# The end of a mixture-of-experts kernel: row blocks of the last weights, and one 1/rms chain for both token blocks

## The chip, the cores and the metric

One core of a Trainium2 chip runs the whole program. The metric is device time in microseconds, as the median of several runs. The profile is of one execution; its times count from the start of its span.

## The reference, cut to what matters

A layer of a language model on 256 tokens of 1024 features, all in float32: a mixer (mLSTM and differential attention), then a mixture of 32 experts, then a final RMS norm. The change touches only the end:

```python
for e in range(N_EXPERTS):                       # 32 experts, 512 hidden features each
    hid = jax.nn.silu(t @ w_eg[e]) * (t @ w_eu[e])
    out = out + gates[:, e:e + 1] * (hid @ w_ed[e])
x = x + out
return rmsnorm(x, normf_g)                       # x * rsqrt(mean(x*x) + eps) * g
```

## The kernel before, in words

All expert weights (32 times 6 MB) stream through SBUF slots of 1 MB. An expert sees only the tokens routed to it: their columns are gathered, multiplied, and the result is added back by a "scatter" matmul with a 0/1 matrix `S_l` into four PSUM banks `acc[j][t]` (j: the half of the 1024 features, t: the block of 128 tokens). These banks hold the sum over all experts and the residual.

Experts are worked on in groups of two or four. A group of four shares the 128 output partitions, 32 slots for each expert. The last group has four, and its down weights `w_ed` are the last thing loaded: 8 MB. Each expert's down weights lie in two slots, `hf` 0 and 1; a slot holds two weight rows k for each partition (k = 2 hf and 2 hf + 1), each of 1024 columns. `load_by_columns` (L776) loads them in pieces: for hf 0 and then hf 1 the first 512 columns of both rows (512 KB for each expert), then for hf 0 the other 512 columns of both rows, then for hf 1 the other 512 columns of row 2 and at last of row 3 (256 KB for each expert and row). All loads are issued on SP's queue (L784), in that order.

On TensorE `down` (L914) multiplies, for the rows `ks` and the halves `js` that it is given, row by row and in a row expert by expert. `keep_warm` (L189) issues matmuls whose result nobody reads. `last_down` (L1132) does for one half j: the rows in pieces with such matmuls between them, then the copy `oH` of the result on ScalarE (L1140), the difference `oL` on VectorE (L1141) and the scatter of both into `acc[j][0]` and `acc[j][1]` (L1144).

Then comes the norm. `square` (L1110, ScalarE) sums the squares of a bank into `ss`; `gain` (L1114, VectorE) writes the bank times the norm's vector `nfb` into `zt`; `rms` (L1117) adds the two halves of a token block and calls `rstd_of` (L161 to L167), a chain of seven small steps between VectorE and ScalarE that gives 1/rms; `scale` (L1123 to L1128) multiplies a quarter of the result with it and issues its write. In the kernel before there is a chain for each token block. The quarter (1, 1) is worked out straight from PSUM in one instruction (L1125). The order of instructions on each engine is set when the kernel is built, by a planner that goes by its own estimate of when an instruction is ready and passes one that isn't; `issue_after` puts an instruction behind a given one of the same engine.

Of the kernel before, what the change touches and what calls it, by code (L numbers as in the profile page):

```python
# [16 lines left out]
OP = mybir.AluOpType  # L17
# [4 lines left out]
NT = 2  # L22
# [15 lines left out]
NWA, NWB, NWZ = 6, 11, 6  # L38
NPJ = 4
NST = 4  # L40
NWARM, NW1, NW2, NW3, NW5 = 9, 2, 10, 4, (8, 4, 4, 3)
NL = 3


# [60 lines left out]
def kernel(ctx: ExitStack, tc: tile.TileContext,  # L105
# [51 lines left out]
    def rstd_of(ss, n, scale, eps, tag="rs"):  # L157

        v, r, y = (cp.tile([P, n], F32, name=tag + c, tag=tag + c, bufs=2 if tag == "rs" else 1) for c in "vry")
        o = cp.tile([P, n], F32, name=tag + "o", tag=tag + "o", bufs=6 if tag == "rs" else 1)  # L160
        behind[1] = V.tensor_scalar(v, ss, scale, eps, op0=OP.mult, op1=OP.add)  # L161
        A.activation(r, v, AF.Ln)  # L162
        behind[0] = A.activation(r, r, AF.Exp, scale=-0.5)  # L163
        V.scalar_tensor_tensor(y, r, -1.0, r, op0=OP.mult, op1=OP.mult)  # L164
        V.tensor_scalar(r, r, 0.5, None, op0=OP.mult)  # L165
        V.tensor_tensor(y, y, v, op=OP.mult)  # L166
        V.scalar_tensor_tensor(o, y, 3.0, r, op0=OP.add, op1=OP.mult)  # L167
        return o
# [12 lines left out]
    def keep_warm(n, pw, after=None):  # L181

        wide = warm[:, None, :].to_broadcast([P, 4, P])
        for _ in range(n):
            if after is None:
                T.matmul(pw, warm, wide, start=True, stop=True)
            else:
                with tc.issue_after(after.ins):
                    after = T.matmul(pw, warm, wide, start=True, stop=True)  # L189
# [586 lines left out]
    def load_by_columns(src, rows):  # L776

        w = [[slot() for _ in rows] for _ in range(2)]
        for hf, k0, k1, j in ((0, 0, 2, 0), (1, 0, 2, 0), (0, 0, 2, 1), (1, 0, 1, 1), (1, 1, 2, 1)):
            for v, e in zip(w[hf], rows):  # L780
                at = [a.rearrange("p (k c) -> p k c", k=2)[:, k0:k1, j * 512:(j + 1) * 512]
                      for a in (v, of_expert(src, e)[:, hf * 2048:(hf + 1) * 2048])]
                with tc.issue_after(loaded[0].ins):
                    loaded[0] = SY.dma_start(*at)  # L784
        return w
# [121 lines left out]
    def down(ws, hT, ojs, ks=range(4), js=range(2)):  # L907
        n = len(ws) // 6
        cap = P // n
        for k in ks:  # L910
            for j in js:
                for i in range(n):
                    c0 = (k % 2) * D + j * 512
                    down_end[0] = T.matmul(ojs[j][i * cap:(i + 1) * cap], hT[:, k, i * cap:(i + 1) * cap],  # L914
                             ws["d", i, k // 2][:, c0:c0 + 512], start=(k == 0), stop=(k == 3))
        return ojs
# [191 lines left out]
    def square(j, t):  # L1108
        sq = mp.tile([P, KD, P], F32, name="xg", tag="xg", bufs=1).rearrange("p k s -> p (k s)")[:, :FF]
        A.activation(sq, acc[j][t], AF.Square, accum_out=ss[:, t, j:j + 1])  # L1110
# [2 lines left out]
        js = slice(j * 512, (j + 1) * 512)  # L1113
        V.tensor_tensor(zt[t][:, js], acc[j][t], nfb[:, js], op=OP.mult)  # L1114

    def rms(t):
        V.tensor_tensor(ss[:, t, 0:1], ss[:, t, 0:1], ss[:, t, 1:2], op=OP.add)  # L1117
        return rstd_of(ss[:, t, 0:1], 1, 1.0 / D, EPS)

    def scale(t, i, E, rf):  # L1120
        z = zt[t][:, i * 512:(i + 1) * 512]
        if E is A:
            A.activation(z, z, AF.Copy, scale=rf)  # L1123
        elif i and t:
            V.scalar_tensor_tensor(z, acc[i][t], rf, nfb[:, i * 512:(i + 1) * 512], op0=OP.mult, op1=OP.mult)  # L1125
        else:
            V.tensor_scalar(z, z, rf, None, op0=OP.mult)  # L1127
        (A if E is A else SY).dma_start(dap(out, t * P * D + i * 512, [[D, P], [1, 512]]), z)  # L1128

    last_end = [up_end[0]]  # L1130

    def last_down(j, pieces):  # L1132
        end = None
        for ks, n in pieces:
            with tc.issue_after((end or last_end[0]).ins):
                down(ws, hT_l, oj, ks, (j,))
                end = down_end[0]
            if n:
                keep_warm(n, warm_to, end)
        A.copy(oH[j], oj[j])  # L1140
        V.tensor_tensor(oL[j], oj[j], oH[j].bitcast(F32), op=OP.subtract)  # L1141
        for o_ in (oH, oL):
            for t in range(NT):
                last_end[0] = T.matmul(acc[j][t], S_l[:, t * P:(t + 1) * P], o_[j], start=False, stop=(o_ is oL),  # L1144
                                       skip_group_check=True)

    last_down(0, (((0, 1), NW5[0]), ((2, 3), 0)))
    for t in range(NT):
        square(0, t)
        gain(0, t)  # L1150
    keep_warm(NW5[1], warm_to, last_end[0])
    last_down(1, (((0, 1), NW5[2]), ((2,), NW5[3]), ((3,), 0)))
    square(1, 0)
    rf = rms(0)
    with tc.issue_after(behind[1].ins):
        gain(1, 0)
    square(1, 1)
    scale(0, 0, V, rf)
    scale(0, 1, V, rf)
    rf = rms(1)  # L1160
    scale(1, 0, A, rf)
    scale(1, 1, V, rf)


# [26 lines left out]
```

## Time and profile before

| | us |
|---|---|
| median of 3 runs | 597.77 (597.15 to 598.19) |
| profiled execution | 597.43 |
| its span | 595.6 |
| last piece of down weights there | 584.17 |
| last output product ends | 591.82 |
| mean granted clock of TensorE | 0.971 |

The span goes from the first to the last record; the time of the execution is 1.8 us longer. The stretch that matters here is the last 30 us: the last loads, the last two down products, the norm and the four writes of 256 KB.

### The profile page before, as it was taken

To read this page: it belongs to the slowest core of one execution; us is meant where nothing else is said; L and a number is where in the kernel's file an instruction comes from. 1 tells how busy PE (TensorE), PEld (TensorE's weight loads), DVE (VectorE), ACT (ScalarE), POOL (GpSimd) and SP (SyncE) were. 2 spreads that over 40 slices of the span, in tenths; PEclk is the share of its full clock that TensorE was granted. 3 is DMA by queue.
4 is the path that set the end of the run, shared out by engine and by line. 5 is a ranking of instruction groups with operands and counts; after the bars stand their busy time and mean duration, and the time that the engine had idled before them with its cause. 6 is when DMAs were issued, how large, how long until landed. Compare 5 with 4: busy or idle time off the path is not lost. (4 is left out here: it accounts for less than half of the span.)

```text
span 595.6 us, 8111 instructions
## 1 busy us (share of the span) xinstructions
PE 529.3 (89%) x3054; PEld 268.4 (45%) x3054; DVE 163.2 (27%) x472; ACT 124.7 (21%) x291; POOL 9.7 (2%) x19
## 2 busy tenths in 40 slices
PE   8999999998999999999889798579798879897683
PEld 6898779795453424343323434123432322431131
DVE  4774788845130202020200200100200010110022
ACT  6675476662100000101001000001000000010032
POOL 0000004001000000000000000000000000000000
PEclk9999999999999999999989989999987889989997
DMA  8955799969899999999999999999999999999992
GB/s 303 389 169 131 239 408 385 388 268 352 300 372 419 390 401 419 419 417 420 419 421 419 420 418 419 423 418 419 419 421 420 419 419 421 419 419 419 406 376 106
DMA packets 42876, 223.77 MB, mean 376 GB/s; under 512 B 3796, under 2 KB 6228, under 8 KB 19156
## 3 DMA queue, kind: packets, MB, share of 16 engines
q1 hardware_dynamic: 42548, 222.89, 93.6%
q8 instruction: 25, 0.41, 0.3%
q10 hardware_dynamic: 288, 0.35, 0.2%
q14 instruction: 15, 0.12, 0.1%
HBM read 221.39 MB, written 1.84 MB: 375 GB/s over the span
## 5 line engine op out<-in xcount | busy, mean ns | idle before, releaser
L897 PE MATMUL pmm<-w,xg 128*32 128x512 f32 (+1 forms) x1024 | 198.8, 615 | 21.8 <-DMA w<-in_w_eu_dram 15.7
L897 PEld LDWEIGHTS pmm<-w,xg 128*32 128x32 f32 (+1 forms) x1024 | 50.9, 122 | 139.6 <-issue 95.1
L914 PE MATMUL pmm<-w,oL 128*32 128x512 f32 (+1 forms) x448 | 97.0, 644 | 11.5 <-ACT oL L836 6.1
L914 PEld LDWEIGHTS pmm<-w,oL 128*32 128x32 f32 (+1 forms) x448 | 29.4, 130 | 71.7 <-issue 47.4
L233 DVE TENSOR_TENSOR wl<-w,wh 128x512 fp32r<-128x512 f32 (+1 forms) x72 | 44.4, 628 | 26.4 <-ACT wh L232 24.0
L843 DVE TENSOR_TENSOR oL<-pmm,oH 128x512 fp32r<-128x512 f32 x20 | 13.8, 692 | 134.2 <-PE pmm L914 104.9
L232 ACT ACTIVATE wh<-w 128x512 fp32r<-128x512 f32 (+1 forms) x72 | 40.8, 580 | 30.2 <-PE pj L263 13.1
L816 PEld LDWEIGHTS pmm<-Gm,x1c 128*128 128x128 f32 x352 | 40.6, 192 | 14.4 <-PE pmm L897 7.7
L816 PE MATMUL pmm<-Gm,x1c 128*128 128x128 f32 x352 | 43.8, 280 | 0.5 <-DVE ctr L989 0.5
L842 ACT CAST oH<-pmm 128x512 fp32r<-128x512 f32 x20 | 11.7, 585 | 120.9 <-PE pmm L914 95.7
L263 PE MATMUL pj<-hL,wh 128*128 128x256 f32 x128 | 36.0, 286 | 0.3 <-DVE hL L245 0.3
L264 PE MATMUL pj<-hH,wl 128*128 128x256 f32 x128 | 35.3, 287 | 0.0
L261 PE MATMUL pj<-hH,wh 128*128 128x256 f32 x128 | 35.3, 286 | 0.0
L817 DVE TENSOR_TENSOR xg<-pmm,cb 128x512 f32<-128x512 f32 (+1 forms) x24 | 15.0, 645 | 72.5 <-PE pmm L897 60.7
L836 ACT COPY oL<-pmm 128x512 f32<-128x512 f32 x10 | 5.8, 585 | 134.7 <-PE pmm L833 134.7
L904 ACT ACTIVATE oL<-pmm,rg 128x512 f32<-128x512 f32 x10 | 6.9, 687 | 91.5 <-PE pmm L897 67.1
L263 PEld LDWEIGHTS pj<-hL,wh 128*128 128x128 f32 x128 | 24.1, 188 | 0.6 <-DVE hL L245 0.5
L264 PEld LDWEIGHTS pj<-hH,wl 128*128 128x128 f32 x128 | 23.6, 188 | 1.4 <-issue 1.2
L261 PEld LDWEIGHTS pj<-hH,wh 128*128 128x128 f32 x128 | 23.8, 189 | 0.2
L833 PE MATMUL pmm<-ca,oH 128*128 128x128 f32 x44 | 7.2, 289 | 16.2 <-DVE oH L829 16.2
L829 DVE SCALAR_TENSOR_TENSOR oH<-oL,rg,pmm 128x512 f32<-128x512 f32 x10 | 11.2, 1119 | 25.8 <-PE pmm L897 22.7
L833 PEld LDWEIGHTS pmm<-ca,oH 128*128 128x128 f32 x44 | 5.0, 150 | 22.3 <-issue 20.1
(344 smaller groups left out, 486.3 us busy)
## 6 DMA issues: line engine op xcount, KB each, us to landing
w<-in_w_eg_dram SPq DMA_DIRECT2D x64, 1024.0 KB, 19.8
w<-in_w_eu_dram SPq DMA_DIRECT2D x64, 1024.0 KB, 19.8
w<-in_w_ed_dram SPq DMA_DIRECT2D x56, 1024.0 KB, 19.8
w<-in_w_in_dram SPq DMA_DIRECT2D x10, 1024.0 KB, 14.9
w<-in_w_ed_dram SPq DMA_DIRECT2D x12, 512.0 KB, 13.0
w<-in_w_out_dram SPq DMA_DIRECT2D x4, 1024.0 KB, 12.8
w<-in_w_ed_dram SPq DMA_DIRECT2D x8, 256.0 KB, 7.3
w<-in_w_in_dram SPq DMA_DIRECT2D x3, 512.0 KB, 7.8
```

The lines of the kernel that those rows point to most:

```text
L232: A.activation(wh, raw, AF.Copy)
L233: V.tensor_tensor(wl, raw, wh.bitcast(F32), op=OP.subtract)
L261: T.matmul(om, wh[:, cs], hH[:, k], start=(k == 0 and m % 2 == 0), stop=False, skip_group_check=True)
L263: T.matmul(om, wh[:, cs], hL[:, k], start=False, stop=False, skip_group_check=True)
L264: T.matmul(om, wl[:, cs], hH[:, k], start=False, stop=(k == KD - 1), skip_group_check=True)
L816: T.matmul(px_[:, i * P:i * P + n], x1c[:, t, k0 + i], G_[:, t], start=(t == 0), stop=(t == NT - 1))
L817: V.tensor_tensor(xg[:, k0:k0 + per, :n], px_.rearrange("p (k s) -> p k s", k=4)[:, :per, :n], cb[:, B_N2 + k0:B_N2 + k0 + per, None].to_b ...
L833: T.transpose(pt[:, k * P:k * P + n], hid[:n, k], ident[:n, :n])
L842: A.copy(oH[:n], oj[:n])
L843: V.tensor_tensor(oL[:n], oj[:n], oH[:n].bitcast(F32), op=OP.subtract)
L897: up_end[0] = T.matmul(p_[i * cap:(i + 1) * cap], xg[:, k, i * cap:(i + 1) * cap], ws[n_, i, k // 4][:, k4 * FF:(k4 + 1) * FF], start=(k = ...
L914: down_end[0] = T.matmul(ojs[j][i * cap:(i + 1) * cap], hT[:, k, i * cap:(i + 1) * cap], ws["d", i, k // 2][:, c0:c0 + 512], start=(k == 0 ...
```

## The change

The last down weights come in another order: rows 0 and 1 (hf 0) whole, 1 MB for each expert; then for hf 1 the first 512 columns of both rows (512 KB each), the other 512 columns of row 2 and those of row 3 (256 KB each). That is 16 issues in place of 20.

On TensorE the order becomes: rows 0 and 1 of half 0, 8 warming matmuls, rows 0 and 1 of half 1, 8 warming matmuls, rows 2 and 3 of half 0, row 2 of half 1, the scatter of half 0, row 3 of half 1, the scatter of half 1. The kernel before did all of half 0 with its scatter and then half 1, with 8, 4, 4 and 3 warming matmuls.

In the norm, `gain` is written ahead of `square` for each bank, the sums of both token blocks are added in one instruction, and one chain of two columns gives both 1/rms. All four quarters are scaled from `zt`: three on VectorE, one on ScalarE. `rms` and the product straight from PSUM go.

```diff
-NWARM, NW1, NW2, NW3, NW5 = 9, 2, 10, 4, (8, 4, 4, 3)
+NWARM, NW1, NW2, NW3, NW5 = 9, 2, 10, 4, (8, 8)
...
-        for hf, k0, k1, j in ((0, 0, 2, 0), (1, 0, 2, 0), (0, 0, 2, 1), (1, 0, 1, 1), (1, 1, 2, 1)):
+        for hf, k0, k1, c0, c1 in ((0, 0, 2, 0, D), (1, 0, 2, 0, 512), (1, 0, 1, 512, D), (1, 1, 2, 512, D)):
             for v, e in zip(w[hf], rows):
-                at = [a.rearrange("p (k c) -> p k c", k=2)[:, k0:k1, j * 512:(j + 1) * 512]
+                at = [a.rearrange("p (k c) -> p k c", k=2)[:, k0:k1, c0:c1]
...
-    def rms(t):
-        V.tensor_tensor(ss[:, t, 0:1], ss[:, t, 0:1], ss[:, t, 1:2], op=OP.add)
-        return rstd_of(ss[:, t, 0:1], 1, 1.0 / D, EPS)
...
-        elif i and t:
-            V.scalar_tensor_tensor(z, acc[i][t], rf, nfb[:, i * 512:(i + 1) * 512], op0=OP.mult, op1=OP.mult)
...
+    def last_down(ks, js, after, n=0):
+        with tc.issue_after(after.ins):
+            down(ws, hT_l, oj, ks, js)
+        if n:
+            keep_warm(n, warm_to, down_end[0])
+        return down_end[0]
+
+    def last_parts(j):
         A.copy(oH[j], oj[j])
         V.tensor_tensor(oL[j], oj[j], oH[j].bitcast(F32), op=OP.subtract)
...
+    def last_scatter(j, after):
+        with tc.issue_after(after.ins):
+            for o_ in (oH, oL):
+                for t in range(NT):
+                    e = T.matmul(acc[j][t], S_l[:, t * P:(t + 1) * P], o_[j], start=False, stop=(o_ is oL),
+                                 skip_group_check=True)
+        return e
+
+    e = last_down((0, 1), (0,), up_end[0], NW5[0])
+    e = last_down((0, 1), (1,), e, NW5[1])
+    e = last_down((2, 3), (0,), e)
+    last_parts(0)
+    e = last_down((2,), (1,), e)
+    e = last_scatter(0, e)
+    e = last_down((3,), (1,), e)
+    last_parts(1)
     for t in range(NT):
+        gain(0, t)
         square(0, t)
-        gain(0, t)
...
+    last_scatter(1, e)
+    for t in range(NT):
+        gain(1, t)
+        square(1, t)
+    V.tensor_tensor(ss[:, :, 0], ss[:, :, 0], ss[:, :, 1], op=OP.add)
+    rf = rstd_of(ss[:, :, 0], NT, 1.0 / D, EPS)
+    for t, i, E in ((0, 0, V), (1, 0, A), (0, 1, V), (1, 1, V)):
+        scale(t, i, E, rf[:, t:t + 1])
```

## Rows read from the trace of the kernel before

**Rows 1.** The page's second part: load rate in 40 equal slices of the span.
```profile
GB/s 303 389 169 131 239 408 385 388 268 352 300 372 419 390 401 419 419 417 420 419 421 419 420 418 419 423 418 419 419 421 420 419 419 421 419 419 419 406 376 106
```

**Rows 2.** Windows; after each engine's busy time: PE clock, DMA share, GB/s.
```profile
554.00:556.00 2.00, 2.00 (x20) 0.56 (x12) 0.00 (x0) 0.00 (x0) 0.00 (x0) 1.00 1.02 422
...
574.00:576.00 2.00, 2.00 (x17) 0.42 (x16) 0.00 (x0) 0.00 (x0) 0.00 (x0) 1.00 1.05 388
```

**Rows 3.** SP's queue by time: start, us of issuing, load issued.
```profile
562.75 0.55 SPq L784 DMA_DIRECT2D w<-in_w_ed_dram  x1
...
573.45 0.33 SPq L784 DMA_DIRECT2D w<-in_w_ed_dram  x1
...
578.85 0.33 SPq L784 DMA_DIRECT2D w<-in_w_ed_dram  x1
```

**Rows 4.** TensorE by time, gate and up products; in brackets the wait before.
```profile
452.91 6.51 PE L897 MATMUL pmm<-w,xg 128*32 128x512 f32 x28 [1.45 <-DMA w<-in_w_eg_dram]
...
552.66 3.63 PE L897 MATMUL pmm<-w,xg 128*32 128x512 f32 x28 [1.46 <-DMA w<-in_w_eu_dram]
...
562.68 3.62 PE L897 MATMUL pmm<-w,xg 128*32 128x512 f32 x26 [1.48 <-DMA w<-in_w_eu_dram]
```

**Rows 5.** The chain that ended last, by time: start, us, what.
```profile
570.41 1.92 PE pmm L914 x16
572.33 1.83 PE pmm L189 x8
...
581.89 1.00 PE pmm L914 x8
```

**Rows 6.** TensorE by time: the scatters, and the wait for the last load.
```profile
576.73 1.46 PE L1144 MATMUL acc<-w,S__3781 128*128 128x512 f32 x4 [0.70 <-ACT w L1140]
577.45 0.30 PEld L1144 LDWEIGHTS acc<-w,S__3781 128*128 128x128 f32 x2 [0.43 <-DVE w L1141]
...
584.17 0.14 PEld L914 LDWEIGHTS pmm<-w 128*32 128x32 f32 x2 [0.46 <-DMA w<-in_w_ed_dram]
...
585.90 1.46 PE L1144 MATMUL acc<-w,S__3781 128*128 128x512 f32 x4 [0.67 <-ACT w L1140]
```

**Rows 7.** ScalarE and VectorE by time: copy, squares, gains, the power chains, scales.
```profile
577.99 0.60 ACT L1110 ACTIVATE xg<-acc 128x512 f32<-128x512 f32 x1 [1.32 <-PE acc L1144]
...
578.71 1.41 DVE L1114 TENSOR_TENSOR w<-acc,w 128x512 f32<-128x512 f32 x2 [1.31 <-ACT xg L1110]
...
585.26 0.58 ACT L1140 CAST w<-pmm 128x512 fp32r<-128x512 f32 x1 [5.86 <-PE pmm L914]
...
587.22 0.60 ACT L1110 ACTIVATE xg<-acc 128x512 f32<-128x512 f32 x1 [1.38 <-PE acc L1144]
587.72 0.19 ACT L1110 ACTIVATION_READ_ACCUMULATOR xg<-acc 128x1 f32 x1
...
588.14 0.15 DVE L161 TENSOR_SCALAR rsv<-ss 128x1 f32<-128x1 f32 x1
...
589.07 0.15 DVE L161 TENSOR_SCALAR rsv<-ss 128x1 f32<-128x1 f32 x1
...
589.25 0.20 ACT L162 ACTIVATE rsr<-rsv 128x1 f32<-128x1 f32 x1 [0.29 <-DVE rsv L161]
...
589.63 0.88 DVE L1127 TENSOR_SCALAR w<-w,rso 128x512 f32<-128x512 f32 x2
...
591.07 0.72 ACT L1123 ACTIVATE w<-w,rso 128x512 f32<-128x512 f32 x1 [1.38 <-DVE rso L167]
```

**Rows 8.** The output: issues on SP's queue, and two windows as in rows 2.
```profile
590.15 0.82 SPq L1128 DMA_DIRECT2D out_dram<-w  x2
...
591.85 0.33 SPq L1128 DMA_DIRECT2D out_dram<-w  x1
```
```profile
591.00:591.50 0.50, 0.00 (x0) 0.00 (x0) 0.46 (x2) 0.43 (x1) 0.00 (x0) 0.50 0.98 360
...
593.50:594.00 0.50, 0.00 (x0) 0.00 (x0) 0.00 (x0) 0.00 (x0) 0.00 (x0) 0.50 1.05 389
```

More of the change, by code (lines that the diff above doesn't have):

```diff
@@ L1128, in scale @@
         (A if E is A else SY).dma_start(dap(out, t * P * D + i * 512, [[D, P], [1, 512]]), z)
[L1130 to L1139, printed above, removed]
+    def last_down(ks, js, after, n=0):
[4 more added lines that the diff above has]
+        return down_end[0]
@@ L1140, in last_down @@
+    def last_parts(j):
         A.copy(oH[j], oj[j])
         V.tensor_tensor(oL[j], oj[j], oH[j].bitcast(F32), op=OP.subtract)
[L1142 to L1147, printed above, removed]
+    def last_scatter(j, after):
[5 more added lines that the diff above has]
+        return e
@@ L1148 @@
+    e = last_down((0, 1), (0,), up_end[0], NW5[0])
[6 more added lines that the diff above has]
+    last_parts(1)
     for t in range(NT):
+        gain(0, t)
         square(0, t)
-        gain(0, t)
[L1151 to L1162, printed above, removed]
+    last_scatter(1, e)
[6 more added lines that the diff above has]
+        scale(t, i, E, rf[:, t:t + 1])
 _BIG = ["x", "w_in", "w_out", "w_eg", "w_eu", "w_ed"]
```

## The prediction, made before the result

> **What bounds the kernel now.** I read the page's load rate first, then the issues on SP's queue with the transfer rate beside them, then TensorE by time, then the chain that ended last, and at the end ScalarE, VectorE and the output. The load rate stays near 419 GB/s for most of the span and sags only in the last slices [rows 1]: the kernel is a stream of weights, and only what follows the stream can be shortened by work on the engines.
>
> SP issues a load when the load eight places earlier has landed, so its issue times are landing times. The last 1 MB piece of the up weights landed at 562.75; the eighth 512 KB piece of the last down weights at 573.45 and the twelfth at 578.85 [rows 3]. That is 10.70/8 = 1.34 us a piece, then 5.40/4 = 1.35: about 388 GB/s, as the window at 574 shows, against 422 for the 1 MB pieces at 554 [rows 2]. The 1 MB pieces have 8 KB in one run for each partition, the column pieces 2 KB. The last piece landed at 584.17, where TensorE's weight load waited for it [rows 6]; the last matmul of the down product ended 1.07 us later, just ahead of the copy at 585.26 [rows 7].
>
> From the copy on, the time is a chain of single steps: copy, difference and scatter (first square at 587.22, 1.96 behind the copy), square, variance (588.14), power, scales (589.63), then the output [rows 7]. The four 256 KB writes move at about 380 GB/s [rows 8]: data from 591.0, 0.85 behind the first issue, and, with the same 0.85 behind the last issue at 591.85 and 512 KB at that rate, to about 594.1.
>
> **The loads.** Rows 0 and 1 of each of the four experts now come as 1 MB, 8 KB for each partition. At the rate of the up weights, 422 GB/s [rows 2], 1.049 MB takes 2.48 us; from 562.75 on the four land at 565.2, 567.7, 570.2 and 572.7. Half columns of rows 2 and 3 follow at 1.35: 578.1. The rest is unchanged in size, 584.17 - 578.85 = 5.32 for 2 MB [rows 3, 6], so row 2 lands at about 580.8 and the last piece at 583.4. Gain: 573.45 - 572.66 = 0.79 us at the end of the loads. Bounds: 0 if long runs bring nothing here, 0.8 if they move as the up weights do; I take 0.79, since size and run are those of the rows that show it. The Trainium skill's page "DMA: Bandwidth & Descriptors" (Specifications) says that from 512 B on a transfer runs at line rate; by that the gain would be 0. The trace differs: 388 against 422 GB/s.
>
> **TensorE.** The first pass needs row 0 of all four experts before row 1, so what it needs first was complete at 562.75 + 4 x 1.34 = 568.1 before and is now at 572.66, and TensorE, which starts at 570.41 [rows 5], waits for it. In the up product, once the last expert's piece was there at 562.68, its four weight rows took 3.62 us [rows 4], so two take 1.81: 574.47. Then, each from the chain [rows 5]: 8 warming matmuls 1.83 (576.30), the pass over the other half 1.92 (578.22), 8 warming 1.83 (580.05), rows 2 and 3 of the first half 1.92 (581.97, weights there since 578.1), row 2 of the second half 1.00 (582.97, weights 580.8). The copy and the difference of the first half lie under that pass. The scatter took 1.46 with 0.43 of waiting for the difference [rows 6]; without the wait 1.03: 584.00. Row 3 takes 1.00: 585.00. By the loads alone it could end at 583.40 + 1.07 = 584.47, so now TensorE decides, and of the 0.79 only 0.24 is left beside the 585.24 of before. The copy could start at 585.02.
>
> **What gets in the way of the copy.** Scatter of the first half ahead of row 3 means that gain and square of the first half fall just where the copy is due. The first gain can start 0.89 behind the scatter's start (1.32 from the scatter's 585.90 to the square at 587.22, less 0.43 [rows 6, 7]): 583.86. A gain and a square of the same block do not run together: the first gain at 578.71 waited for the square, started at 577.99, to end, and two gains took 1.41 [rows 7]. With gain first: gain 583.86 to 584.55, square 584.58 to 585.27. ScalarE's next is either the copy or the second square. The order that is built isn't the written one: the second block's variance step ran at 589.07, ahead of the first block's scales at 589.63, which are written first [rows 7]; so an instruction that is ready passes one that isn't. Taken at the times just worked out, the first square is ready (584.58) before the copy (585.02), and at 585.27 both copy and second square are, of which the copy is written first. I take that middle order: copy at 585.29, as before (585.26). Bounds: 585.02 with the copy first, 586.01 with both squares first.
>
> **The tail, counted from the copy.** The scatter is unchanged: block 0 ready at 1.96. Gain 1.98 to 2.67 (0.69 each), second gain to 3.37, second square 3.40 to 4.09: the gain's 0.70 now lies ahead of each square, where a square came first before. Variance at 4.32 (0.23 behind the square's end, as 588.14 behind 587.91 [rows 7]). From variance to scales the first block took 1.49 (588.14 to 589.63), but its logarithm was late: a free ScalarE takes it up 0.18 behind the variance (589.07 to 589.25), that is at 588.32, and here the other square's 0.60, begun at about 587.93, held it to 588.53. Without these 0.2 it is 1.30 [rows 7]: scales at 5.62. Before, they began at 4.37. Two columns in place of one cost nothing: these steps are 0.15 to 0.2 us whatever they hold. The longer chain is covered by nothing.
>
> What is given back: no second chain, and the three products on VectorE are 0.44 each (0.88 for two), the last ending at 6.94 beside 6.56 before; ScalarE's 0.72 is off the path. The writes: the first was issued 0.52 behind the scales' start, and data flowed 0.85 later [rows 7, 8]. Before, two writes went out while the second chain ran and two after it. Now all four follow one another within 0.9 us, so the rate decides: 5.62 + 0.52 + 0.85 + 2.77 (1 MB at 380 GB/s) = 9.76, against 594.1 - 585.26 = 8.84. Tail: +0.92. If the writes overlapped fully, the bound is the last issue at about 7.0 and its 2.25 to the end of data: 9.25, +0.4.
>
> **Sum**, against the profiled execution (span 595.6, time 597.43): copy +0.03, tail +0.92, so +0.95 to 598.4. That execution lies 0.34 below the median of the three runs (597.77), so about 598.7 as a median. A difference under 0.2% (1.2 us) can't be told from none, so this counts as no change.
>
> **Rivals.**
> *The copy first* (15%): the copy at 585.02, +0.7, 598.5. For it: it is the earlier one in the text. Against it: it must be ready within 0.7 us of the first gain.
> *Both squares first* (22%), the one on the other side: the copy at 586.01, 0.75 later than before, +1.7, 599.4. It decides from a copy later than about 585.55. For it: if the order is built with TensorE's row 3 a little later than I have it, by a load or by the matmuls, the second square is ready first. Against it: at the times of this trace the copy is ready 0.25 us before the second square.
> *The long runs bring nothing* (10%): all from the first pass on is 0.79 later, since TensorE's chain hangs on the fourth expert: +1.7, 599.5. The page's rule above would give this. Against it: rows 2.
> *TensorE's clock falls while it waits for the fourth expert* (5%): one idle stretch of about 1.3 us. Once, behind a wait of 1.45, the same 28 matmul records took 6.51 in place of 3.63 [rows 4], 2.9 more; +3.8, 601.6. Against it: behind waits as long at 552.66 and 562.68 they ran at full speed [rows 4].
> *Gain and square run together* (5%): the tail loses 0.72, +0.2, 598.0. Against it: rows 7. The page "PSUM — Partial Sum Buffer" (Terms) of the Trainium skill says that two engines on one bank at once is an error, reads included; the wait at 578.71 agrees.
> *Something of the stream that I don't see gets shorter* (3%): faster by more than 1.2 us would need the loads to end 2 us earlier and TensorE to follow; nothing in the rows offers that.
>
> **Numbers.** The forecast has 40%. Its own range, 598.2 to 599.2, comes from 0.3 us on each of the scatter, the scales' start and the writes. Slower by over 0.2% are most of the both-squares case, the long-runs case, the clock's, and a fifth of the forecast's: 0.40. Faster 0.04, the same 0.56. For 8 in 10, the range goes from below the lower cases (597.6) to above both squares and the long runs (599.9), and leaves out the clock.
>
> **What would show it.** On SP's queue: four issues of 1 MB, and the last landing near 583.4. On TensorE: a wait of about 1.3 us for the fourth expert's rows and none for a load after it, last down product ending near 585.0. On ScalarE: square, copy, square. A scale start 5.6 behind the copy; four writes without a gap. The prediction is wrong if TensorE still waits for the last load, if the first pass doesn't wait, or if the writes hide behind the chain.

## The result, and the profile after

| | before | after |
|---|---|---|
| median, us | 597.77 (597.15 to 598.27, 7 runs) | 601.0 (599.17 to 602.96, 7 runs) |
| profiled execution, us | 597.43 | 599.17 |

The ratio is 1.0051 (95%: 1.003 to 1.0073): slower, and above the range that was given. The profiled execution is the shortest of its seven. By itself it is 1.74 us longer than the one before, 0.29%. So there are two differences to explain: 1.74 us between two profiles, and the 1.83 us by which the median lies above its own profile.

The page of after, the load rate in 40 slices, which answers [rows 1]:

```profile
GB/s 297 389 178 134 220 409 387 391 270 345 307 376 417 386 424 419 416 419 420 419 419 421 421 419 419 421 420 420 417 421 419 421 417 421 419 421 419 421 333 71
```

The slice of 406 before is now at 421, and the last two are lower (333 for 376, 71 for 106): the stream keeps its rate longer and is over sooner. SP's queue by time (start, us of issuing, load) and two windows of after, for [rows 2, 3]:

```profile
572.60 0.33 SPq L784 DMA_DIRECT2D w<-in_w_ed_dram  x1
...
577.95 0.33 SPq L784 DMA_DIRECT2D w<-in_w_ed_dram  x1
```

```profile
572.00:574.00 2.00, 1.38 (x10) 0.38 (x10) 0.00 (x0) 0.00 (x0) 0.00 (x0) 1.00 1.04 374
574.00:576.00 2.00, 2.00 (x10) 0.70 (x8) 0.00 (x0) 0.00 (x0) 0.00 (x0) 1.00 1.06 391
```

The fourth expert's rows landed at 572.60, and at 577.95 the 6 MB were there that had been there at 578.85 [rows 3]. In the first window TensorE is busy 1.38 of 2 us, the wait for the fourth expert; its clock stays at 1.00, the level of 2.4 GHz.

TensorE by time, after. In brackets the wait and its releaser:

```profile
562.62 3.62 PE L897 MATMUL pmm<-w,xg 128*32 128x512 f32 x26 [1.44 <-DMA w<-in_w_eu_dram]
...
572.62 1.90 PE L914 MATMUL pmm<-w 128*32 128x512 f32 x10 [1.21 <-DMA w<-in_w_ed_dram]
...
582.69 1.37 PE L1139 MATMUL acc<-w,S__3781 128*128 128x512 f32 x4
583.99 1.06 PE L914 MATMUL pmm<-w 128*32 128x512 f32 x8
586.52 1.46 PE L1139 MATMUL acc<-w,S__3781 128*128 128x512 f32 x4 [1.47 <-ACT w L1132]
```

Row 3 of the second half ran 583.99 to 585.05 without a wait: TensorE, not the loads, sets the end of the down product. Then the scatter waits 1.47 us for the copy on ScalarE, where it waited 0.67 before [rows 6]. ScalarE and VectorE by time, after (for [rows 7]):

```profile
584.59 0.60 ACT L1110 ACTIVATE xg<-acc 128x512 f32<-128x512 f32 x1 [2.04 <-DVE w L1114]
...
585.31 0.60 ACT L1110 ACTIVATE xg<-acc 128x512 f32<-128x512 f32 x1
...
585.89 0.58 ACT L1132 CAST w<-pmm 128x512 fp32r<-128x512 f32 x1
588.57 0.60 ACT L1110 ACTIVATE xg<-acc 128x512 f32<-128x512 f32 x1 [2.09 <-DVE w L1114]
...
589.28 0.60 ACT L1110 ACTIVATE xg<-acc 128x512 f32<-128x512 f32 x1
```

```profile
583.87 1.29 DVE L1114 TENSOR_TENSOR w<-acc,w 128x512 f32<-128x512 f32 x2 [0.59 <-PE acc L1139]
...
587.78 1.29 DVE L1114 TENSOR_TENSOR w<-acc,w 128x512 f32<-128x512 f32 x2 [0.59 <-PE acc L1139]
...
590.20 0.17 DVE L161 TENSOR_SCALAR rsv<-ss 128x2 f32<-128x2 f32 x1
...
591.53 1.28 DVE L1121 TENSOR_SCALAR w<-w,rso 128x512 f32<-128x512 f32 x3
```

Both squares of the first half stand ahead of the copy, which could have started at about 585.07 and starts at 585.89. The writes, after (for [rows 8]):

```profile
592.04 1.37 SPq L1122 DMA_DIRECT2D out_dram<-w  x3
...
592.28 0.36 ACTq L1122 DMA_DIRECT2D out_dram<-w  x1
```

To compare executions, I count from one event that the change doesn't touch, called the anchor: the last up weights are there and the last 26 matmuls of the up product start, at 562.68 before [rows 4] and 562.62 after. From there:

| us behind the step ahead | before | after |
|---|---|---|
| anchor to copy of the second half | 22.58 | 23.27 |
| copy to first scales | 4.37 | 5.64 |
| first scales to the execution's time | 7.80 | 7.64 |
| anchor to the execution's time | 34.75 | 36.55 |

So +0.69, +1.27, -0.16: 1.80 in all, less 0.06 for the anchor itself. A difference of 0.3 us between two profiles can also come from loads that land later: the kernel before with a steady up product (below) does the same work behind the anchor and takes 35.06.

### The profile page after: what moved, and what is told of

Same layout as the page of the kernel before. It is cut to its first block, busy times and chain, and to the rows that moved or that the text cites. A ratio compares the mean times of both kernels' runs of the same rounds, so it can differ in the third digit from the quotient of the medians.

```text
span 597.4 us, 8086 instructions
## 1 busy us (share of the span) xinstructions
PE 531.8 (89%) x3051; PEld 269.6 (45%) x3051; DVE 162.9 (27%) x467; ACT 124.3 (21%) x289; POOL 9.2 (2%) x19
## 4 chain that ended last, share of the span: by engine, by line
DMA 58%; PE 37%; DVE 2%; ACT 1%; issue 1%; SPq 0%; DVEq 0%; ACTq 0%
DMA w<-in_w_eu_dram 20%; DMA w<-in_w_ed_dram 20%; DMA w<-in_w_eg_dram 17%; PE pmm L897 8%; PE pmm L914 4%; PE pmm L816 3%; PE pj L264 2%; PE pj L263 2%; PE pj L261 2%; PE pj L274 1%; PE pj L275 1%; PE acc L612 1%; PE pj L273 1%; PE acc L613 1%; PE acc L614 1%; DMA xs<-in_x_dram 1%
## 5 line engine op out<-in xcount | busy, mean ns | idle before, releaser
L897 PE MATMUL pmm<-w,xg 128*32 128x512 f32 (+1 forms) x1024 | 201.4, 623 | 19.2 <-DMA w<-in_w_eu_dram 14.2
```

The source lines that it names most:

```text
L897: up_end[0] = T.matmul(p_[i * cap:(i + 1) * cap], xg[:, k, i * cap:(i + 1) * cap], ws[n_, i, k // 4][:, k4 * FF:(k4 + 1) * FF], start=(k = ...
```

## The experiments

The edits are against after, unless before is named. A ratio is worked out from all runs, against the kernel before in the same measurement, and can differ from the quotient of the medians by up to 0.0011. Four theories stand in the expectations by letter, on why the median is higher than the profile explains. A: in some executions TensorE's clock falls in the wait for the fourth expert. B: the writes, or the loads with 8 KB runs, take a varying time. C: the clock falls in the waits inside the last up product, in both kernels. D: the new load order costs something in the usual execution that the profiled one doesn't show.

**After again.** No edit.

> The changed kernel again, to see which executions are the long ones. The profiled one came out at the both-squares case (599.2), the median 1.8 us above it. Theory A (TensorE's clock): in some executions the granted clock falls to its lower level while TensorE waits about 1.2 us for the fourth expert's rows, and the passes and warming matmuls behind it run at half speed; times again spread over 599 to 603, and if the profile catches a long one, the windows behind 572 show a clock of 0.5 and a pass of 16 records takes near 3.8 us in place of 1.9. Theory B (the four writes in one heap, or the loads of 8 KB runs, vary in length): same spread, but a long profile shows full clock behind 572 and a later last landing or a longer output.

601.27 (598.52 to 602.9, 12 runs) against 598.45 (596.23 to 601.14, 35 runs of the kernel before): 1.0043 (1.0023 to 1.0063). The kernel before now spreads over 5 us too, where its first seven runs had spread over 1.1. In this profile TensorE was late in the up product:

```profile
561.96 5.32 PE L897 MATMUL pmm<-w,xg 128*32 128x512 f32 x26 [1.44 <-DMA w<-in_w_eu_dram]
...
571.39 2.47 PE L914 MATMUL pmm<-w 128*32 128x512 f32 x16 [0.41 <-PEq L1040]
```

```profile
562.00:564.00 2.00, 2.00 (x12) 0.51 (x16) 0.00 (x0) 0.00 (x0) 0.00 (x0) 0.61 1.06 438
564.00:568.00 4.00, 3.28 (x18) 0.69 (x10) 0.63 (x1) 0.00 (x0) 0.00 (x0) 0.77 1.00 416
```

The same 26 records took 5.32 us in place of 3.62, at a granted clock of 0.61 in the window from 562; the engine had just waited 1.44 us for the up weights. Being late took away its wait for the fourth expert, so the 1.7 us were absorbed: anchor to time is 36.56, as in the first profile (36.55). This execution, 598.52, is the shortest of its twelve, so it doesn't show a long one.

**Rows 0 and 1 by column halves.** The new order of work stays, the 8 KB runs go.

```diff
-  for hf, k0, k1, c0, c1 in ((0, 0, 2, 0, D), (1, 0, 2, 0, 512), ...
+  for hf, k0, k1, c0, c1 in ((0, 0, 2, 0, 512), (0, 0, 2, 512, D), (1, 0, 2, 0, 512), ...
```

> Only the loads of rows 0 and 1 go back to column halves (512 KB each, first halves of all experts, then second halves); everything else as changed. TensorE's first pass then finds its weights at 570.4 (they land by 568.1) and has no wait, the later passes wait at most 0.7 us. Theory A: the spread is gone (within 1 us) and the median falls to about 599, both squares still ahead of the copy. Theory B with the 8 KB loads: the spread is gone too. Theory B with the writes: the spread stays, 599 to 603. The last landing goes back to about 584.2 in either case, if long runs gave 0.8 us.

599.18 (597.92 to 601.86): 1.0023 (1.0005 to 1.0042). That is 0.20%, or 1.2 us, below after in the same measurement, which is the side of theory D, but the intervals overlap. In its profile the clock fell in the up product as well (26 records in 6.53 us), and the first pass began at 572.10 without a wait for a load, so it doesn't test what the wait is worth. It spreads as the others do, without the 8 KB runs, and the kernel before spreads so without the new writes either: against both forms of B. SP's queue, where the first 6 MB are there:

```profile
577.76 0.33 SPq L784 DMA_DIRECT2D w<-in_w_ed_dram  x1
```

That is 16.30 behind the anchor, where it is 15.33 in after and 16.17 before: without the 1 MB pieces the gain of the loads is gone.

**The norm alone.** In the kernel before, only the end is changed: gain ahead of square, one chain, four products with the norm's vector ahead of it.

```diff
+        gain(0, t)
         square(0, t)
-        gain(0, t)
...
-    square(1, 0)
-    rf = rms(0)
...
+    for t in range(NT):
+        gain(1, t)
+        square(1, t)
+    V.tensor_tensor(ss[:, :, 0], ss[:, :, 0], ss[:, :, 1], op=OP.add)
+    rf = rstd_of(ss[:, :, 0], NT, 1.0 / D, EPS)
```

> The kernel before with only the new norm (gain ahead of square, one chain, three products on VectorE from SBUF); loads and TensorE as before. The prediction's term for the tail: +0.9 us, median 598.7, scales 5.6 us behind the copy, no spread. Theory A: no spread, since no wait was added on TensorE. Theory B with the writes: spread of some 3 us as in the changed kernel.

599.84 (597.41 to 602.19): 1.0022 (1.0002 to 1.0042). It spreads by 4.8 us though TensorE has no new wait: against A. Anchor to time is 35.96, 1.21 more than before. ScalarE and VectorE of this kernel:

```profile
585.61 0.59 ACT L1138 CAST w<-pmm 128x512 fp32r<-128x512 f32 x1 [5.47 <-PE pmm L914]
```

```profile
587.51 1.29 DVE L1114 TENSOR_TENSOR w<-acc,w 128x512 f32<-128x512 f32 x2 [0.59 <-PE acc L1142]
...
591.26 1.28 DVE L1125 TENSOR_SCALAR w<-w,rso 128x512 f32<-128x512 f32 x3
```

The scales start 5.65 behind the copy, 1.28 more than before, and the time is 7.40 behind the scales, 0.40 less: the tail costs 0.88, where 0.92 had been forecast. The other 0.33 lie ahead of the copy, which waits for TensorE, and TensorE for loads that were later in this execution: the 6 MB are there 16.47 behind the anchor, 16.17 before. The new norm costs its 1.28 with either order of the loads.

**The wait filled.** Six warming matmuls behind the third expert's row 0 keep TensorE busy where it waits for the fourth. `first_rows` issues the matmuls of the given (row, expert) in that order behind the instruction given.

```diff
+    e = first_rows([(0, 0), (0, 1), (0, 2)], up_end[0])
+    for _ in range(6):
+        with tc.issue_after(e.ins):
+            e = T.matmul(warm_to, warm, warm[:, None, :].to_broadcast([P, 4, P]), start=True, stop=True)
+    e = first_rows([(0, 3), (1, 0), (1, 1), (1, 2), (1, 3)], e)
+    keep_warm(NW5[0], warm_to, e)
```

> The changed kernel with six more warming matmuls between the third and the fourth expert's first row, where TensorE waited for the fourth expert; their results are not read. Theory A: no idle stretch, the clock stays at its upper level, the spread is gone and the median is about 599.3 (the time of the fast executions of the changed kernel, at most 0.2 later). Theory B: the spread stays and the median is near 601.

601.18 (598.58 to 604.12): 1.0044 (1.0022 to 1.0065). Neither median nor spread came down: against A. The one profile of this version shows what the fill costs when TensorE is late already (26 records in 5.29 us):

```profile
570.97 1.06 PE L1146 MATMUL pmm<-w 128*32 128x512 f32 x6 [0.40 <-PEq L1040]
571.96 1.47 PE L1153 MATMUL pmm<-warm 128*128 128x512 bf16 x6
573.36 1.90 PE L1146 MATMUL pmm<-w 128*32 128x512 f32 x10
```

The weights are there and the six matmuls run first; the pass starts at 573.36, 11.79 behind the anchor, where it was 10.00 in after.

**Before and after with a steady last up product.** Five warming matmuls in each of six waits of that product, in the kernel before and in the one after. The product is written out row by row k and expert by expert i, and behind its matmul (k, i) stands:

```diff
+            for _ in range(5 if k % 4 == 0 and i < 3 else 0):
+                with tc.issue_after(e.ins):
+                    e = T.matmul(fill_to, warm, warm[:, None, :].to_broadcast([P, 4, P]), start=True, stop=True)
```

> The kernel before with five warming matmuls in each of the six waits for an expert's weights of the last up product; their results are not read. So far three of six profiles show TensorE's clock at its lower level through that product (26 records in 5.3 to 6.5 us in place of 3.6), which puts everything behind it 1.7 to 2.9 us later in whatever kernel. Theory C: that is where the executions differ; here the product takes 3.6 us in every execution, the times lie within about 1.5 us and the median is 1 to 1.5 us under that of the kernel before. If executions differ for another reason the spread stays at 4 to 5 us.

> The same warming matmuls in the last up product, in the changed kernel; everything else as changed. Theory C: every execution is like the profiled ones, near 36.6 us behind the last up weights' landing, so 598.2 to 599.4, and against the kernel of the first run of this group the difference is that of the profiled executions, 1.7 to 2.0 us. Theory A (the clock falls in the wait for the fourth expert's down rows): long executions of 601 to 603 remain.

Before: 599.18 (596.55 to 600.85), 1.0008 (0.999 to 1.0027). After: 599.41 (598.46 to 601.97), 1.0013 (0.9997 to 1.0028). In both profiles the 26 records took 3.62 us, and in after the wait for the fourth expert was 1.20 with the clock at 1.00 behind it, as in the first profile:

```profile
573.14 1.90 PE L914 MATMUL pmm<-w 128*32 128x512 f32 x10 [1.20 <-DMA w<-in_w_ed_dram]
```

But the spread of the kernel before stayed, and its median lies 0.79 above that of the unfilled one (598.39), not 1 to 1.5 under it: C is a real delay in single executions, and not what spreads them. Anchor to time is 35.06 and 36.55. So the two profiles differ by 1.49, but the two medians by 0.23, where 1.7 to 2.0 had been expected. Resampling the two sets of twelve runs gives an interval of -0.7 to 2.0 us for that difference: it neither bears the steps out nor refutes them.

**The loads and the order without the new norm, and all fills.** After's loads and order of TensorE; the norm of before with its two chains and squares ahead of gains; six warming matmuls in the wait for the fourth expert and six between the passes, in place of eight and eight; and the steady up product. The fills are those shown above; the norm's edit is:

```diff
-        gain(0, t)
         square(0, t)
+        gain(0, t)
...
-    for t in range(NT):
-        gain(1, t)
-        square(1, t)
-    V.tensor_tensor(ss[:, :, 0], ss[:, :, 0], ss[:, :, 1], op=OP.add)
-    rf = rstd_of(ss[:, :, 0], NT, 1.0 / D, EPS)
...
+    square(1, 0)
+    rf = rms(0)
+    with tc.issue_after(behind[1].ins):
+        gain(1, 0)
+    square(1, 1)
...
+    rf = rms(1)
```

> The changed loads and TensorE order with the two chains and products of the kernel before, squares ahead of gains, the first warming matmuls moved into the wait for the fourth expert's rows (six and six in place of eight and eight), and the warming matmuls in the last up product. By the steps: row 3 ends about 1.3 us earlier than in the changed kernel (584.4 where the last up weights land at 562.6), the copy finds ScalarE free, the tail is that of the kernel before (8.8 us from copy to the end of data): about 0.7 us under the kernel before at its best, 596.0 to 597.0, and 1.5 to 2 under its median.

597.68 (596.32 to 599.24): 0.9981 (0.9963 to 0.9999), the lowest median of any version here, and the only interval below 1, by very little. It lies 0.71 under the median of before, where 1.5 to 2 had been expected. Against after with the steady product it is 1.73 lower in the median and 1.76 from anchor to time. Its profile is no better than that of before: anchor to time 34.79 against 34.75. TensorE and ScalarE:

```profile
583.56 0.14 PEld L914 LDWEIGHTS pmm<-w 128*32 128x32 f32 x2 [0.41 <-DMA w<-in_w_ed_dram]
```

```profile
584.65 0.58 ACT L1146 CAST w<-pmm 128x512 fp32r<-128x512 f32 x1 [0.36 <-PE pmm L914]
```

With TensorE earlier, the last load is waited for again. It lands 21.27 behind the anchor, 21.49 before [rows 4, 6]: at that point 0.22 is left of the loads' gain, because the first 512 KB piece behind the 1 MB ones took 1.89 us here (issues at 572.24 and 574.13), where it took 1.32 in after. The copy is 22.36 behind the anchor, 22.58 before, and the scales follow it by 4.36, 4.37 before. The 0.22 is lost again behind the last write (the last section has the reason): from the scales to the time it is 8.07 here, 7.80 before.

**The copy first.** The squares of the first half go behind the copy on ScalarE; `last_parts` returns the copy.

```diff
-    last_parts(1)
+    c = last_parts(1)
...
-        square(0, t)
+        with tc.issue_after(c.ins):
+            square(0, t)
```

> The changed kernel with one edit: both squares of the first half are put behind the copy of the second half on ScalarE. The copy then starts when row 3 is done: 0.8 us earlier, at 585.07 where it started at 585.89 in the changed kernel's profile, and all behind it too; median 600.4. If the copy's place on ScalarE were not what delays it, no change.

600.19 (599.06 to 602.74): 1.0033 (1.0014 to 1.0052). ScalarE by time:

```profile
585.84 0.59 ACT L1132 CAST w<-pmm 128x512 fp32r<-128x512 f32 x1 [2.65 <-PE pmm L914]
586.32 0.60 ACT L1110 ACTIVATE xg<-acc 128x512 f32<-128x512 f32 x1
```

The copy waits for TensorE alone and is 22.61 behind the anchor (563.23 in this profile), 0.66 earlier than in after; anchor to time is 35.91, 0.64 less. So the order on ScalarE is what delays the copy in after; 0.8 had been expected.

**The old norm alone.** The version with all fills, but without the fills in the two products' waits, and with after's eight and eight warming matmuls; the norm's edit is the diff shown there.

> The changed loads and TensorE order with the norm of the kernel before (two chains, squares ahead of gains). By the steps: the squares of the first half no longer stand behind gains, so the copy starts 0.6 us earlier than in the changed kernel, and the tail is 0.9 us shorter; that leaves +0.2 against the kernel before, so about the same time. Theory D (the loads or TensorE's wait cost something in the usual execution that the profiled ones don't show, 1 us or more): it stays 1 us or more slower than the kernel before.

598.86 (597.13 to 600.96): 1.0017 (1.0001 to 1.0033). Anchor to time 35.10: 0.35 more than before, 1.45 less than after. ScalarE:

```profile
588.43 0.58 ACT L1138 CAST w<-pmm 128x512 fp32r<-128x512 f32 x1
```

The copy starts right behind the second square, 22.57 behind the anchor (565.86), 22.58 before; the scales follow it by 4.45 and the time these by 8.08, 7.80 before. So the new loads and order bring nothing up to the copy, they cost 0.28 at the end, and the norm is the greater loss. The median is 1.05 above that of before, which is what D had named; by the ratio it is 1.0 us, with an interval of 0.1 to 2.0 that also holds the +0.2 expected.

**After a third time.**

> The changed kernel once more, for its median and a third profile. By the steps seen in the profiles it should be 1.8 us over the kernel before; the two measurements so far gave 3.2 and 2.8 with intervals from 1.4 to 4.4. If it comes out near 1.8, the steps account for all of it; at 2.8 or more, 1 us stays unexplained. In the profile the wait for the fourth expert's rows is 1.2 us where the last up product ran at the full clock, and none where it ran at the lower one.

599.85 (597.79 to 601.79): 1.0028 (1.0011 to 1.0045). The median is 2.04 above that of before, the ratio gives 1.7 us: near the 1.8 of the steps. Its profiled execution, 601.72, was the second longest of the twelve, so here a usual long one can be read. TensorE:

```profile
565.14 3.62 PE L897 MATMUL pmm<-w,xg 128*32 128x512 f32 x26 [1.44 <-DMA w<-in_w_eu_dram]
...
575.15 1.90 PE L914 MATMUL pmm<-w 128*32 128x512 f32 x10 [1.22 <-DMA w<-in_w_ed_dram]
```

All is 2.52 us late at the anchor; from there to the time it is 36.58, as in the other three profiles of the changed kernel (36.55, 36.56, 36.55). In these four the part behind the anchor doesn't vary, as B would have it, and this measurement does without D. Column halves and the old norm lean to D's side by about 1 us, within their intervals, so D is not excluded. The lateness of this execution is there early on. SP's queue of after and then of this run, at the same load of gate weights:

```profile
80.43 0.33 SPq L773 DMA_DIRECT2D w<-in_w_eg_dram  x1
```

```profile
83.25 0.33 SPq L773 DMA_DIRECT2D w<-in_w_eg_dram  x1
```

And the windows from 10 to 15 us of after and of this run (PE, PEld, DVE, ACT, POOL, then the granted clock):

```profile
10.00:15.00 5.00, 5.00 (x44) 5.00 (x43) 4.22 (x8) 4.78 (x10) 0.00 (x0) 1.00 1.06 384
```

```profile
10.00:15.00 5.00, 5.00 (x34) 5.00 (x33) 3.74 (x7) 3.46 (x9) 0.00 (x0) 0.71 1.06 386
```

In this execution the clock was at its lower level (1.2 GHz) for part of the first 15 us, and 34 matmuls were done where 44 were.

**Square ahead of gain.** Each square is written ahead of its gain in both halves; one chain and four products stay.

```diff
-        gain(0, t)
         square(0, t)
+        gain(0, t)
...
-        gain(1, t)
         square(1, t)
+        gain(1, t)
```

> The changed kernel with each square written ahead of its gain; one chain as changed. The squares of the first half end 0.7 us sooner and let the copy start about 0.6 us earlier. In the tail the squares end 0.7 us sooner too, but on VectorE the sum of the squares stands behind both gains, and the second gain now waits for the second square: scales again near 5.6 us behind the copy. So 0.6 us faster than the changed kernel in all. If gains could run beside squares, the tail would lose 0.7 us too.

598.77 (597.24 to 600.15): 1.0008 (0.9991 to 1.0024). Anchor to time 35.82, 0.73 less than after. ScalarE and VectorE:

```profile
585.85 0.59 ACT L1132 CAST w<-pmm 128x512 fp32r<-128x512 f32 x1
```

```profile
588.61 1.41 DVE L1114 TENSOR_TENSOR w<-acc,w 128x512 f32<-128x512 f32 x2 [1.37 <-ACT xg L1110]
...
591.45 1.28 DVE L1121 TENSOR_SCALAR w<-w,rso 128x512 f32<-128x512 f32 x3
```

The copy now starts as soon as the second square ends, 22.59 behind the anchor (563.26): 0.68 of the gain is here. Behind it nothing changed: scales 5.60 behind the copy, where they were 5.64. The squares run earlier, but the two gains wait for them, the sum on VectorE stands behind the second gain, and that 0.70 is paid in another place.

All profiles side by side. The load is that of the gate weights shown above; its issue time, the clock of the first 20 us and the anchor are of the profiled execution, and the ratios are each against the kernel before in the same measurement:

| version | ratio (95%) | load issued | clock 0 to 20 | anchor | anchor to time |
|---|---|---|---|---|---|
| before | | 80.33 | 1.00 | 562.68 | 34.75 |
| after | 1.0051 (1.0030 to 1.0073) | 80.43 | 1.00 | 562.62 | 36.55 |
| after again | 1.0043 (1.0023 to 1.0063) | 80.64 | 1.00 | 561.96, late | 36.56 |
| column halves | 1.0023 (1.0005 to 1.0042) | 80.04 | 1.00 | 561.46, late | 36.97 |
| norm alone | 1.0022 (1.0002 to 1.0042) | 81.49 | 0.91 | 562.70 | 35.96 |
| wait filled | 1.0044 (1.0022 to 1.0065) | 80.25 | 1.00 | 561.57, late | 38.35 |
| before, steady | 1.0008 (0.9990 to 1.0027) | 80.32 | 1.00 | 561.89 | 35.06 |
| after, steady | 1.0013 (0.9997 to 1.0028) | 81.88 | 0.91 | 563.15 | 36.55 |
| old norm, all fills | 0.9981 (0.9963 to 0.9999) | 80.74 | 1.00 | 562.29 | 34.79 |
| copy first | 1.0033 (1.0014 to 1.0052) | 80.76 | 1.00 | 563.23, late | 35.91 |
| old norm | 1.0017 (1.0001 to 1.0033) | 84.18 | 0.83 | 565.86 | 35.10 |
| after, third time | 1.0028 (1.0011 to 1.0045) | 83.25 | 0.91 | 565.14 | 36.58 |
| square first | 1.0008 (0.9991 to 1.0024) | 81.77 | 0.91 | 563.26 | 35.82 |

"Late" marks the four profiles in which the 26 records behind the anchor took 5.05 to 6.53 us.

## Why the prediction was wrong

Three steps failed: the copy's place on ScalarE, the end of the writes by a smaller amount, and the way from one execution to a median. The last of them took the result out of the range; the profiled execution lies within it.

*The middle order on ScalarE failed.* "I take that middle order: copy at 585.29" became 585.89: the built order is square, square, copy, the rival on the other side (22%, copy at 586.01, 599.4 as a median and so 599.1 for the profiled execution; 599.17 came). The working said that an order "taken at the times just worked out" would put the copy in between, and gave as the rival's condition a copy later than about 585.55. On the chip row 3 ended at 585.05, so the condition wasn't met, and the copy was last all the same. The order is not that of readiness on the chip: it was settled when the kernel was built, and by which estimates no row of the trace shows. The chances should have been spread over the orders that the planner can give, and not put on the one that the traced times favour. With the copy forced ahead, anchor to time falls by 0.64.

*The sum was made a median by adding 0.34.* The profiled execution came out at 599.17, 0.8 above the forecast for it (598.4): 0.60 from the copy, 0.02 from the scales and 0.17 from the writes. That 599.17 lies so near the both-squares rival's 599.1 is in part luck: its copy came 0.12 earlier than the rival had it, and its writes have the same 0.17 missing. The rest of the miss, 601.0 against 598.7, is that this execution was the shortest of its seven, and the median 1.83 above it. The three runs of before lay within 1.04 us, and nothing was put into the range for how executions spread; in 99 later runs of the same kernel, in three measurements, they reach from 596.23 to 601.48. Of sets of seven drawn from these 99, fewer than one in a hundred lie as close together as the first seven (1.12 us); why these did is not known. Three measurements of the changed kernel gave 1.0051, 1.0043 and 1.0028: the profile's 1.80 us from the anchor on (0.30%) lies in the last two intervals and at the edge of the first. The first median is then probably in part chance; whether a part of its excess belongs to the change, as theory D has it, is open, as the intervals are 2 us wide. What spreads the executions is not known either.

*The end of the writes.* From the scales to the time 0.33 less was forecast, and 0.16 less came. With 20 loads the new norm has 0.40 less (7.40 in the norm alone, 7.39 in column halves, 7.80 before), so this product and these writes are a little better than forecast. The 16 loads add about 0.25 behind the last write, a term that the sum doesn't have; the last section shows where.

The other steps held. *The loads*: 0.79 forecast, 0.84 measured behind the anchor, where 6 MB have landed (577.95 - 562.62 against 578.85 - 562.68). In other executions the same point lies 15.32 to 15.96 behind the anchor with 16 loads and 16.17 to 16.47 with 20, so a gain is shown; between the means it is 0.75. From 562.62 the four 1 MB pieces took 9.98 us, 420 GB/s; the column pieces with 2 KB runs moved at 388 before and 391 after. The Trainium skill's page "DMA: Bandwidth & Descriptors" (Specifications) gives line rate from 512 B on; these rows don't agree with that. Whether it is the run or the size of the piece (512 KB) that counts was not told apart. *TensorE*: wait for the fourth expert to 572.62 (572.66 forecast), first pass 574.52 (574.47), second 578.22 (578.22), warming matmuls to 580.05 (580.05), row 3 to 585.05 (585.00). That TensorE eats the loads' gain is what the version with the old norm shows: its last matmul ends 22.43 behind the anchor, 22.56 before, and the copy starts at 22.57, 22.58 before. *The clock* stayed at 1.00 behind the wait in all five profiles where TensorE waited there (1.14 to 1.22 us each), as the 5% for that rival had it. *Gain, then square*: the first square starts 0.72 behind the first gain, and copy to scales took 5.64 (5.62 forecast). A chain step on two columns took 0.17 (590.20) where it took 0.15 on one, so nearly nothing; more columns were not tried. That each pair of reads of a bank goes in the written order is shown from both sides: square behind gain here, gain behind square in the version with squares first, with the same 5.6 at the end.

*Where the gain went.* Long runs free 0.84 us of loads; TensorE, which now waits for rows of all four experts ahead of its first pass, lets 0.13 of it through (its last matmul ends 22.43 behind the anchor, and 22.56 before), and two squares take 0.82 at the copy. The single chain saves instructions on VectorE, but the 1/rms of both blocks starts only when the second block's gain and square are done, while before the first block's scales and writes ran meanwhile: +1.27 on the path. With the square ahead of the gain the scales still start 5.60 behind the copy, so it isn't their order that costs this. Of the 1.27 the shorter products and writes give 0.40 back, and the end behind the last write takes 0.25 of that.

## What to carry to other kernels

Two chains that overlap can be shorter than one that does both: the merged one starts with its last input, and what stands ahead of it on the engines that share its inputs is paid in full. Where work is moved next to the instruction that the path needs, fix the order by hand, and don't trust that the earlier one is taken first. Before a change of 0.2% is predicted or judged, look at how far executions of the same kernel lie apart, and compare profiles from one event that the change doesn't touch.

## What was not expected of the hardware

Executions of one kernel on one core lie up to 5 us apart (596.42 to 601.48 in one measurement of the kernel before). In the 13 profiles the five with a granted clock of 0.83 or 0.91 over the first 20 us are the five with the latest issue of the load shown above (81.49 to 84.18; the other eight 80.04 to 80.76). That holds in all 13, but wasn't tried by a change at the start of the kernel; the anchors, 561.46 to 565.86, follow it only in part.

In the last up product TensorE waits six times for weights, mostly 1.36 to 1.48 us, and between most of these waits it has about 1.04 us of work. In seven of the ten profiles without fills there the granted clock fell to its lower level in that product, after among them (0.50 from 552 to 556). In four of the seven it was low over the last 26 records, which then took 5.05 to 6.53 us. In the three profiles with fills it didn't fall there, and in none of the five with the single wait of 1.14 to 1.22 us that the change made did it fall in or behind that wait.

The end behind the last write differs by version. From the end of the last issue of a write on SP's queue to the end of the span, us, in all 13 profiles:

| | 20 loads | 16 loads |
|---|---|---|
| old norm | 3.46, 3.51 | 3.75, 3.75 |
| new norm | 3.73, 3.75 | 3.97 to 3.98 (seven) |

The trace shows where the 0.25 go. There SP takes eight waits for transfers, one behind the other in a fixed order, and one whose transfer has long landed still takes 0.06 us. In after the last write is the second of the eight: that wait ends 2.77 behind the issue, and six more follow to 3.14. In column halves it is the sixth: that wait ends at 2.76, and two more follow to 2.88. Four waits more behind the last landing make 0.25 us. That the number of loads ahead decides the place of the last write is read from these two orders, and no other number was tried.
